# Decoding the gathered tile one tile of gate matrices later, with eight of its gathers among the last parked blocks

## The chip, the cores and the metric

One core of one Trainium2 chip. The time is device microseconds of an execution, the median over several runs. TensorE (PE) does the matmuls, VectorE (DVE) and ScalarE (ACT) the element-wise work, GpSimd (POOL) issues the gathers, and SyncE's queue (SP) issues all other DMAs.

## The reference, cut to what matters

Two transformer blocks over 512 tokens of width 1024, all in float32. What the change touches is the expert layer of the first block (`peer`), for which each of 8 heads chooses 16 of 128 × 128 experts for each token:

```python
q = (xc @ w_query).reshape(c, PEER_HEADS, 2, D_HALF)
sc = jnp.einsum('chpd,hpkd->chpk', q, sub_keys)
sv, si = lax.top_k(sc, PEER_TOPK)
...
fv, fi = lax.top_k(cand, PEER_TOPK)
idx = jnp.take_along_axis(cidx, fi, axis=-1)
g = jax.nn.softmax(fv, axis=-1)
a = jax.nn.gelu(jnp.einsum('chkd,cd->chk', u_tab[idx], xc))
return jnp.einsum('chk,chkd->cd', g * a, v_tab[idx])
```

## The kernel before, in words

The 512 tokens are four tiles of 128. The expert layer does them in two ways.

**Tile 0 is gathered.** Its 128 choices for each token are turned into an index tile `ix` and weights `gw0`. Then 256 gathers follow (`gather_steps`, L482): for each head 16 rows of `u_experts` (tile `gu`, L488) with a dot product on VectorE (L490), a gelu and a product for the head (L493, L494), and 16 rows of `v_experts` (tile `gv`, L497), each added to `hres` by VectorE (L499). Each gather moves 128 rows of 4 KB, 512 KB. They share four buffers, so POOL runs at most four gathers ahead of VectorE.

**Tiles 1 to 3 are computed densely.** All experts' hidden values are made (`h_block`, L469, or `h_stage`, L697: 24 matmuls of 384 columns for a block of 128 experts), multiplied by a gate matrix that is zero where an expert was not chosen, and multiplied with `v_experts` (`v_stage`, L718). The gate matrices are built beforehand (`gate_matrix`, L615), 16 tokens at a time, so eight for each tile, named (t, q): for each token a one-hot column `og` (two instructions on ScalarE at L633 and L634, or one on VectorE at L630, by the table `ON_DVE`), a one-hot block `oj` for eight tokens (VectorE, L620), a matmul for each token (L636), a copy by ScalarE (`stg`, L638) and a store to DRAM (`wdr`, L639).

**Parked blocks.** TensorE has little to do while choices are made and gate matrices are built, so 68 of the 128 hidden blocks are computed there and stored (`park_blocks`, L477): a load of 512 KB, a split into `whi` by ScalarE (L132) and `wlo` by VectorE (L134), 24 matmuls into `hps`, a gelu (`hg`, L474), a store of 192 KB. Sixteen go along with the choices (L545), two with each decode (L574), one or two behind each gate matrix (L640, by `PARKS`), and the rest, four, behind the last (L653).

**Decoding** (`decode`, L564) turns a tile's choices into what its gate matrices or gathers need: comparisons and sums on VectorE (`eq`, L584 to L589), an exponential on ScalarE (L596), whose table load and the load back to the gelu's table (at L474) come with it, and for tile 0 the index tile (L603, L604). It is called for tile 1 ahead of the first gate matrix, and for the others at the places in the table `DECODE`. Once tile 0 is decoded, each gate matrix is followed by `GATH[t]` gathers (L642).

In this stage the order of instructions on each engine is the framework's scheduler's: it takes ready instructions by their order in the program, so that later work can fill gaps that it foresees. The waits on buffers and data are as in the program.

**The long loop** (L743) runs in an order written out by hand: for each of the 128 blocks loads ahead, splits ahead (`dsplit`, L680), a share of the gathers left by `RATE` (0.74 for a parked block, 2.6 for another), the next block's hidden values with the multiplication `hw` (L709), and this block's `v_stage`. The matmuls of the last three blocks come after the loop (L760).

Of the kernel before, what the change touches and what calls it, by code (L numbers as in the profile page):

```python
# [25 lines left out]
PARKED = [n for n in range(NLEAD, 128)  # L26
          if (n + 1 - NLEAD) * NPARK // (128 - NLEAD) > (n - NLEAD) * NPARK // (128 - NLEAD)]
PARKS = ((), (2, 1), (2, 2), (2, 1))
GATH = (0, 1, 3, 3)
RATE = (0.74, 2.6)  # L30
DECODE = {(1, 1): 0, (1, 4): 2, (2, 3): 3}
ON_DVE = ((), (0, 2), (0, 1, 2), (0, 1, 2))
INV_FREQ = [1.0, 0.1939227432012558, 0.03760603070259094, 0.007292664609849453,
            0.0014142135623842478, 0.00027424818836152554, 5.3182957344688475e-05, 1.0313385246263351e-05]
# [9 lines left out]
def body(ctx: ExitStack, tc: tile.TileContext, A: dict, out: bass.AP):  # L44
# [377 lines left out]
    with ExitStack() as st:  # L422
# [54 lines left out]
        def park_blocks():  # L477
            for k, n in enumerate(PARKED):
                SY.dma_start(park[k], h_block(n))
                yield  # L480

        def gather_steps():  # L482
            a = ga
            for h in range(8):
                hs = slice(16 * h, 16 * h + 16)
                for s_ in range(16 * h, 16 * h + 16):
                    u = gt.tile([128, D], F32, name="gu", tag="gu")
                    GP.indirect_dma_start(out=u, out_offset=None, in_=A["u_experts"],  # L488
                                          in_offset=bass.IndirectOffsetOnAxis(ap=ix[:, s_:s_ + 1], axis=0))
                    V.tensor_tensor_reduce(out=u, in0=u, in1=xtok, scale=1.0, scalar=0.0,  # L490
                                           op0=OP.mult, op1=OP.add, accum_out=a[:, s_:s_ + 1])
                    yield
                SC.activation(a[:, hs], a[:, hs], AF.Gelu)  # L493
                V.tensor_tensor(a[:, hs], a[:, hs], gw0[:, hs], op=OP.mult)  # L494
                for s_ in range(16 * h, 16 * h + 16):
                    v = gt.tile([128, D], F32, name="gv", tag="gu")
                    GP.indirect_dma_start(out=v, out_offset=None, in_=A["v_experts"],  # L497
                                          in_offset=bass.IndirectOffsetOnAxis(ap=ix[:, s_:s_ + 1], axis=0))
                    V.scalar_tensor_tensor(hres[:, 0, :], v, a[:, s_:s_ + 1], hres[:, 0, :],  # L499
                                           op0=OP.mult, op1=OP.add)  # L500
                    yield

        parks = park_blocks()
        gathers = gather_steps()

        def spread(gen, n):
            for _ in range(n):
                next(gen, None)

        with mix as s1:  # L510
# [104 lines left out]
            def gate_matrix(t, q, sT, nT):  # L615
                stg = rw.tile([128, 128, TG], F32, name="stg", bufs=2)
                for c in range(TG // 8):
                    t8 = q * TG + 8 * c
                    oj = rw.tile([128, 8, 128], F32, name="oj", bufs=2)
                    V.tensor_tensor(oj, io[:, None, :].to_broadcast([128, 8, 128]),  # L620
                                    sT[:, 1, t8:t8 + 8, None].to_broadcast([128, 8, 128]), op=OP.is_equal)
                    for e in range(2):
                        pool, tag = ((psw, "wps"), (pmm, "mm"))[e]
                        ps = pool.tile([128, 4, 128], F32, name="wps", tag=tag)
                        for k in range(4):
                            tok = t8 + 4 * e + k
                            dve = k in ON_DVE[t]
                            og = rw.tile([128, 128], F32, name="og", tag="ogv" if dve else "oga", bufs=6)
                            if dve:
                                V.tensor_scalar(og, io, sT[:, 0, tok:tok + 1], sT[:, 2, tok:tok + 1],  # L630
                                                op0=OP.is_equal, op1=OP.mult)
                            else:
                                SC.activation(og, io, AF.Abs, bias=nT[:, 0, tok:tok + 1])  # L633
                                SC.activation(og, og, AF.Relu, scale=nT[:, 2, tok:tok + 1],  # L634
                                              bias=sT[:, 2, tok:tok + 1])
                            PE.matmul(ps[:, k, :], lhsT=oj[:, 4 * e + k, :], rhs=og)  # L636
                        o = 8 * c + 4 * e
                        SC.activation(stg[:, :, o:o + 4].rearrange("p i t -> p t i"), ps, AF.Copy)  # L638
                SY.dma_start(wdr[(t - 1) * (128 // TG) + q], stg)  # L639
                spread(parks, PARKS[t][q % 2])  # L640
                if 0 in ahead:
                    spread(gathers, GATH[t])  # L642

# [3 lines left out]
            for t in range(1, NT):  # L647
                for q in range(128 // TG):
                    if (t, q) in DECODE:
                        n = DECODE[t, q]  # L650
                        ahead[n] = decode(n)
                    gate_matrix(t, q, *ahead[t])
            spread(parks, NPARK)  # L653

        dn = st.enter_context(tc.tile_pool(name="dn", bufs=2, reuse_waits="tile"))
# [466 lines left out]
```

## Time and profile before

| | us |
|---|---|
| median of 3 runs | 2280.13 (2277.22 to 2281.48) |
| the profiled execution | 2283.24 |
| its span, first to last instruction | 2281.5 |
| TensorE busy | 2222.8 (97%) |
| VectorE busy | 1500.5 (66%) |
| ScalarE busy | 999.0 (44%) |
| POOL busy | 357.4 (16%) |
| mean granted TensorE clock | 0.991 |

The stage of the gate matrices takes about 545 to 860 us of the span: the store of the first gate matrix is issued at 578.34, that of (2,0) at 678.49, of (3,0) at 784.14, and of the last at 855.04. The long loop follows up to about 1660. Busy times are the union of an engine's instructions; a matmul's end is modelled, so that short gaps between matmuls don't show as idle. The granted clock is a mean over the stretch, in shares of full speed.

### The profile page before, as it was taken

How to read it: one execution, taken by the hardware profiler on the slowest of the kernel's cores; microseconds unless marked ns; L12 is line 12 of the kernel's file. 1: busy time of each engine (PE TensorE's matmuls, PEld its weight loads, DVE VectorE, ACT ScalarE, POOL GpSimd, SP SyncE). 2: the span in 40 equal slices, each digit the busy share in tenths (PEclk: the TensorE clock that was granted, in tenths of full speed). 3: DMA queues.
4: the chain of work that ended last, by engine and by line, in shares of the span. 5: the costliest groups of instructions: out<-in, count | busy, mean ns of one | idle time of the engine just before them, and what ended most of it. 6: DMA issues, size and time to landing. Idle time of an engine off the chain costs nothing.

```text
span 2281.5 us, 30213 instructions
## 1 busy us (share of the span) xinstructions
PE 2222.8 (97%) x11337; PEld 1924.1 (84%) x11337; DVE 1500.5 (66%) x3010; ACT 999.0 (44%) x1655; POOL 357.4 (16%) x261
## 2 busy tenths in 40 slices
PE   7999998999999999999999999999999999999998
PEld 6888887888899998888888888888876778888886
DVE  5663445999999995777777777777774655333323
ACT  5474224333997773333333333333353464323221
POOL 0000000000122421333333333333200000000000
PEclk9999999999999999999999999999999999999999
DMA  4303233443687998989989888988732112333331
GB/s 157 93 29 121 83 95 112 125 123 107 236 313 289 368 334 278 320 296 310 322 303 324 301 311 302 331 317 306 251 112 68 56 61 91 98 95 99 94 101 65
DMA packets 177572, 444.82 MB, mean 195 GB/s; under 512 B 15249, under 2 KB 84241, under 8 KB 174353
## 3 DMA queue, kind: packets, MB, share of 16 engines
q1 hardware_dynamic: 140560, 308.65, 40.3%
q0 software_dynamic: 36864, 134.23, 16.7%
q8 instruction: 89, 1.46, 0.2%
q14 instruction: 59, 0.48, 0.1%
HBM read 402.19 MB, written 40.63 MB: 194 GB/s over the span
## 4 chain that ended last, share of the span: by engine, by line
PE 84%; DVE 6%; ACT 5%; issue 4%; DMA 2%; POOL 0%; SPq 0%; DVEq 0%; ACTq 0%; POOLq 0%
PE mm L138 13%; PE mm L139 13%; PE mm L140 13%; PE acc L138 7%; PE acc L140 7%; PE acc L139 7%; PE hps L140 6%; PE hps L138 6%; PE hps L139 6%; PE wps L636 2%; ACT stg L638 1%; PE pv L363 1%; PE sc L914 1%; PE pv L940 1%; DVE wlo L134 1%
## 5 line engine op out<-in xcount | busy, mean ns | idle before, releaser
L132 ACT ACTIVATE whi<-wraw 128x1024 fp32r<-128x1024 f32 x232 | 241.8, 1045 | 532.6 <-PE mm L139 304.2
L134 DVE TENSOR_TENSOR wlo<-wraw,whi 128x1024 fp32r<-128x1024 f32 x232 | 278.5, 1203 | 271.3 <-ACT whi L132 269.0
L138 PE MATMUL hps<-x2h,whi 128*128 128x384 f32 x1024 | 347.5, 339 | 2.0 <-ACT whi L132 1.8
L140 PE MATMUL hps<-x2h,wlo 128*128 128x384 f32 x1024 | 344.8, 337 | 1.4 <-DVE wlo L134 0.9
L139 PE MATMUL hps<-x2l,whi 128*128 128x384 f32 x1024 | 343.8, 336 | 0.0
L488 POOL DMA_INDIRECT gu<-in_u_experts_dram,ix x128 | 176.7, 1380 | 900.7 <-PE wps L636 584.7
L138 PE MATMUL acc<-whi,hh 128*128 128x512 f32 x768 | 301.4, 392 | 9.4 <-ACT hh L119 9.3
L140 PE MATMUL acc<-whi,hl 128*128 128x512 f32 x768 | 302.7, 394 | 0.6 <-DVE hl L120 0.6
L139 PE MATMUL acc<-wlo,hh 128*128 128x512 f32 x768 | 301.2, 392 | 0.0
L688 DVE TENSOR_TENSOR wlo<-wraw,whi 128x1024 fp32r<-128x1024 f32 x188 | 228.2, 1222 | 84.0 <-ACT whi L686 83.8
L686 ACT ACTIVATE whi<-wraw 128x1024 fp32r<-128x1024 f32 x188 | 196.1, 1052 | 117.5 <-issue 51.9
L497 POOL DMA_INDIRECT gv<-in_v_experts_dram,ix x128 | 178.4, 1394 | 380.7 <-DVE hres L499 264.4
L138 PEld LDWEIGHTS hps<-x2h,whi 128*128 128x128 f32 x1024 | 193.0, 188 | 5.5 <-ACT whi L132 2.1
L139 PEld LDWEIGHTS hps<-x2l,whi 128*128 128x128 f32 x1024 | 192.8, 188 | 2.8
L140 PEld LDWEIGHTS hps<-x2h,wlo 128*128 128x128 f32 x1024 | 192.7, 188 | 2.2 <-DVE wlo L134 1.1
L138 PEld LDWEIGHTS acc<-whi,hh 128*128 128x128 f32 x768 | 144.8, 189 | 42.8 <-ACT hh L119 14.9
L119 ACT ACTIVATE hh<-hw 128x384 fp32r<-128x384 f32 x128 | 67.2, 525 | 248.1 <-DVE hw L709 248.1
L140 PEld LDWEIGHTS acc<-whi,hl 128*128 128x128 f32 x768 | 144.8, 189 | 35.2 <-DVE hl L120 5.3
L139 PEld LDWEIGHTS acc<-wlo,hh 128*128 128x128 f32 x768 | 144.8, 189 | 28.8
L499 DVE SCALAR_TENSOR_TENSOR hres<-gv,ga,hres 128x1024 f32<-128x1024 f32 x128 | 164.0, 1281 | 3.7 <-DMA gv<-in_v_experts_dram,ix 2.4
L490 DVE CUSTOM_DVE_ANT_0 gu<-gu,xtok 128x1024 f32<-128x1024 f32 x128 | 153.9, 1218 | 0.0
L139 PE MATMUL mm<-x4l,whi 128*128 128x512 f32 (+1 forms) x384 | 143.3, 374 | 0.0
(320 smaller groups left out, 4135.4 us busy)
## 6 DMA issues: line engine op xcount, KB each, us to landing
wraw<-in_u_cols_dram SPq DMA_DIRECT2D x128, 512.0 KB, 6.1
wraw<-in_v_experts_dram SPq DMA_DIRECT2D x128, 512.0 KB, 6.0
wraw<-in_w_in_dram SPq DMA_DIRECT2D x50, 512.0 KB, 3.6
wdr<-stg SPq DMA_DIRECT2D x24, 1024.0 KB, 5.3
wt<-wdr SPq DMA_DIRECT2D x16, 1536.0 KB, 11.4
park<-hg SPq DMA_DIRECT2D x68, 192.0 KB, 3.9
hg<-park SPq DMA_DIRECT2D x68, 192.0 KB, 6.2
wraw<-in_w_gate_dram SPq DMA_DIRECT2D x22, 512.0 KB, 3.5
```

The costliest lines, as they stand in the source:

```text
L119: SC.activation(hi, ps, AF.Copy)
L132: SC.activation(hi, raw, AF.Copy)
L134: V.tensor_tensor(lo, raw, f(hi), op=OP.subtract)
L138: PE.matmul(ps, lhsT=ah, rhs=bh, start=start, stop=False)
L139: PE.matmul(ps, lhsT=ah, rhs=bl, start=False, stop=False)
L140: PE.matmul(ps, lhsT=al, rhs=bh, start=False, stop=stop)
L488: GP.indirect_dma_start(out=u, out_offset=None, in_=A["u_experts"], in_offset=bass.IndirectOffsetOnAxis(ap=ix[:, s_:s_ + 1], axis=0))
L490: V.tensor_tensor_reduce(out=u, in0=u, in1=xtok, scale=1.0, scalar=0.0, op0=OP.mult, op1=OP.add, accum_out=a[:, s_:s_ + 1])
L497: GP.indirect_dma_start(out=v, out_offset=None, in_=A["v_experts"], in_offset=bass.IndirectOffsetOnAxis(ap=ix[:, s_:s_ + 1], axis=0))
L499: V.scalar_tensor_tensor(hres[:, 0, :], v, a[:, s_:s_ + 1], hres[:, 0, :], op0=OP.mult, op1=OP.add)
L686: SC.activation(hi, raw, AF.Copy)
L688: V.tensor_tensor(lo, raw, f(hi), op=OP.subtract)
```

## The change

`GATH` is the number of gathers behind each gate matrix of tile t, and `DECODE` names the gate matrix (t, q) ahead of which a tile is decoded. Tile 0's decode moves from (1, 1) to (2, 1), tile 3's from (2, 3) to (2, 4). The gathers behind gate matrices become 3 × 7 + 3 × 8 = 45 where there were 7 + 24 + 24 = 55, and eight more are placed in pairs behind the last four parked blocks. Ahead of the long loop there are then 53 for 55.

```diff
-GATH = (0, 1, 3, 3)
+GATH = (0, 0, 3, 3)
 RATE = (0.74, 2.6)
-DECODE = {(1, 1): 0, (1, 4): 2, (2, 3): 3}
+DECODE = {(1, 4): 2, (2, 1): 0, (2, 4): 3}
...
                     gate_matrix(t, q, *ahead[t])
+            for _ in range(4):
+                spread(parks, 1)
+                spread(gathers, 2)
             spread(parks, NPARK)
```

## Rows read from the trace of the kernel before

**Rows 1.** The page: each engine's busy time, share of the span, instructions.

```profile
PE 2222.8 (97%) x11337; PEld 1924.1 (84%) x11337; DVE 1500.5 (66%) x3010; ACT 999.0 (44%) x1655; POOL 357.4 (16%) x261
```

**Rows 2.** Stretches: length, each engine's busy time (instructions), granted clock, DMA share, GB/s.

```profile
566.00:668.60 102.60, 93.29 (x575) 89.34 (x576) 95.33 (x177) 96.74 (x198) 24.22 (x17) 0.94 0.71 253
584.00:590.00 6.00, 4.61 (x23) 4.14 (x23) 4.72 (x15) 5.90 (x12) 3.89 (x4) 0.65 0.48 137
590.00:596.00 6.00, 6.00 (x33) 6.00 (x32) 6.00 (x12) 5.23 (x14) 3.27 (x2) 0.78 0.87 292
...
723.00:784.00 61.00, 61.00 (x407) 60.62 (x407) 60.86 (x110) 45.62 (x84) 26.70 (x19) 1.00 0.99 361
845.00:860.00 15.00, 15.00 (x99) 14.85 (x98) 6.76 (x11) 7.93 (x10) 1.68 (x1) 1.00 0.84 300
860.00:892.00 32.00, 32.00 (x179) 31.14 (x178) 11.83 (x14) 12.38 (x18) 0.00 (x0) 1.00 0.79 251
```

**Rows 3.** TensorE's waits, 566 to 600, 600 to 683, 683 to 860: total, times, longest.

```profile
PE hps L138 <- ACT whi L132: 1.8, 1, 1.8
PE wps L636 <- DVE og L630: 1.4, 2, 0.9
...
PE wps L636 <- ACT og L634: 5.6, 7, 1.1
...
PE wps L636 <- DVE og L630: 1.0, 3, 0.7
```

**Rows 4.** ScalarE's waits, 566 to 669.

```profile
ACT stg L638 <- PE wps L636: 3.0, 4, 1.9
ACT hg L474 <- PE hps L140: 2.3, 2, 1.3
```

**Rows 5.** VectorE in order of time, at tile 0's and tile 3's decode: start, length.

```profile
572.06 0.22 DVE L577 TENSOR_SCALAR ab<-fi 128x128 uint32<-128x128 uint32 x1
...
582.85 1.25 DVE L620 TENSOR_TENSOR oj<-io,sT 128x1024 f32<-128x1024 f32 x1
...
682.19 0.29 DVE L566 CAST sif<-si 128x256 bf16<-128x256 uint32 x1
...
705.52 0.40 DVE L591 TENSOR_TENSOR sel<-eq 128x128 f32<-128x128 bf16 x1
```

**Rows 6.** Groups of instructions from 540 to 870: count, busy us, mean ns.

```profile
L132 ACT ACTIVATE whi<-wraw 128x1024 fp32r<-128x1024 f32 x49 | 51.4, 1060 | 48.4 <-PE hps L139 47.8
L499 DVE SCALAR_TENSOR_TENSOR hres<-gv,ga,hres 128x1024 f32<-128x1024 f32 x23 | 29.6, 1287 | 0.3
L474 ACT ACTIVATE hg<-hps 128x384 f32<-128x384 f32 x51 | 24.3, 477 | 4.9 <-issue 2.5 <-PE hps L140 2.3
L596 ACT ACT_TABLE_LOAD x4 | 5.1, 1283 | 0.1
L474 ACT ACT_TABLE_LOAD x4 | 5.1, 1283 | 0.1
L596 ACT ACTIVATE gw<-gw 128x128 f32<-128x128 f32 x4 | 1.2, 310 | 3.1 <-DVE gw L595 3.0
```

**Rows 7.** Parked blocks' matmuls in two stretches: PE, PEld and ACT busy (instructions).

```profile
545.00:561.00 16.00, 16.00 (x93) 15.69 (x91) 2.02 (x5) 1.00 0.26 82
566.00:668.60 102.60, 61.72 (x316) 55.60 (x317) 6.28 (x13) 0.94 0.71 253
```

**Rows 8.** The gathers' dot products (L490, two instructions each) up to 680.

```profile
566.00:680.00 114.00, 19.13 (x32) 0.94 0.74 267
```

**Rows 9.** VectorE in order of time, at the end of the long loop.

```profile
1645.93 2.60 DVE L499 SCALAR_TENSOR_TENSOR hres<-gv,ga,hres 128x1024 f32<-128x1024 f32 x2
...
1654.31 1.23 DVE L688 TENSOR_TENSOR wlo<-wraw,whi 128x1024 fp32r<-128x1024 f32 x1 [1.30 <-ACT whi L686]
1655.45 0.55 DVE L709 TENSOR_TENSOR hw<-hg,wt 128x384 f32<-128x384 f32 x1
```

**Rows 10.** TensorE in order of time, at the end of the long loop.

```profile
1656.64 0.50 PE L138 MATMUL acc<-whi,hh 128*128 128x512 f32 x1 [2.10 <-ACT hh L119]
```

## The prediction

> **What bounds the kernel now.** I read the page first, for the engine that the span belongs to [rows 1]: TensorE is marked busy for 97% of it, VectorE for 66%. So a change pays only where TensorE stands still or runs below its rate. The change lies in the stage of the gate matrices (545 to 860 us), so I cut that stage by what TensorE does in it [rows 2]. From 723 to 784, in the second tile (t=2), TensorE is busy in all 61.00 us, at 0.150 us for each of its 407 matmuls. From 566 to 668.6, the first tile (t=1), it is busy 93.29 of 102.60, and 575 matmuls at 0.150 us would take 86.3. So about 16 us are lost there, by idle time, by the lower clock (mean grant 0.94), and by small gaps that the modelled ends cover.
>
> [...]
>
> Who holds TensorE in the first tile? The waits [rows 3] say: up to 600 us, ScalarE's split of a weight once (1.8) and VectorE's one-hot rows (1.4); from 600 to 683, ScalarE's one-hot rows alone (5.6 in 7 waits). ScalarE is busy 96.74 of 102.60 us in this tile [rows 2] and waits for TensorE only 3.0 and 2.3 us [rows 4]. So ScalarE is what this tile runs at, with one place where VectorE was late: the decode of tile 0 occupies VectorE from 572.06 to 582.85, where the one-hot block `oj` of the next gate matrix at last starts [rows 5]. [...] In the second and third tiles VectorE is full (60.86 of 61.00) and TensorE loses nearly nothing; its one wait for VectorE from 683 to 860 is 1.0 us [rows 3].
>
> **The change part by part.**
>
> *Decode of tile 0, and its two parked blocks, out of the first tile.* ScalarE is relieved of two table loads (1.283 each) and an exponential (0.3): 2.9 us. Each of the two parked blocks that the decode issues takes with it a split (1.06) and a gelu (0.48), so 3.1 us [rows 6]. Where ScalarE sets the pace the tile ends 2.9 + 3.1 = 6.0 us earlier. Its two issue DMAs each (a 512 KB load, a 192 KB store) go along on SP's queue; they now stand behind the stores of eight more gate matrices, with nothing but later loads and stores behind them.
>
> *ScalarE's own waits in the first tile.* Of its waits for TensorE [rows 4], 1.9 us is the start of the tile and stays. The others (1.1 for the gate matrices' results, 2.3 for parked blocks) come from TensorE being late. With two parked blocks less it should not be: I take 3.4, the whole, because the waits are for exactly the work that thins out; the ends are 0 and 3.4.
>
> *The same two blocks in the second tile.* There TensorE has no room. A parked block is 24 matmuls at 0.172 us (93 in 16.00) [rows 7], so two cost 2 × 4.13 = +8.3 us. If instead they are taken into the first tile as filler, ScalarE pays 3.1 for them there and the 8.3 is gone. No row shows a parked block running ahead of its place: from 566 to 668.6 there are 316 such matmuls, 13 blocks, and the program places 15 between the first and the last gate matrix of the tile. So I take the full 8.3; the low end is 3.1.
>
> *The decode in its new place.* It needs some 10.8 us of VectorE, from 572.06 to 582.85 [rows 5], in a tile where VectorE is full. What is queued behind it is the next `oj` and `og`, and TensorE behind those. The nearest row is tile 3's decode in the same tile: it began at 682.19, well ahead of its place, and all of TensorE's waits for VectorE in that stretch come to 1.0 us. I take +1.0. The ends are 0 (taken wholly into the first tile) and 6.6: what the decode cost where it stood, 3.2 us of waits (1.8 and 1.4 [rows 3]) and the slow pieces behind them. [...]
>
> *Gathers.* Ten fewer stand ahead of the last parked blocks (45 for 55), so VectorE has some 12 us less to do before them, at 1.2 to 1.3 each; that offsets the decode there. Sixteen dot products ran by 680 [rows 8], where the program had placed ten by the end of the second tile's first gate matrix, so gathers are moved freely into VectorE's gaps, and none held TensorE. I take 0, within −1 and +1. POOL's queue carries nothing but gathers here, so its longer wait for the index tile stops nothing else.
>
> *Eight gathers among the last four parked blocks.* VectorE idles 8.2 of 15 us from 845 to 860 and 20.2 of 32 from 860 to 892 [rows 2]; eight updates at 1.287 [rows 6] are 10.3. They also bring 4.2 MB into 47 us in which the DMA engines are busy 0.84 and 0.79 of the time: 9.1 us are free for 11.6 at the 361 GB/s of the second tile. The 2.5 us over would come late to the long loop's first loads; TensorE has three blocks to do meanwhile, so I take 0, with ends 0 and 2.5.
>
> *Two gathers less before the long loop.* The loop's rate gives 206 places. With 53 done it needs 203 of them, not 201, so one gather falls after block 124's matmuls and one before the multiplication `hw` for block 126. VectorE's idle time before 1654.31 takes the first. The second comes between the split at 1654.31 and `hw` at 1655.45 [rows 9], behind which TensorE already waited 2.10 us at 1656.64 [rows 10]. Two such updates take 2.60, so this is +1.3 us; ends 0 and 2.6.
>
> **Sum:** −6.0 − 3.4 + 8.3 + 1.0 + 0 + 0 + 1.3 = +1.2 us. The profiled execution took 2283.24 (span 2281.5 and 1.7 around it), 3.11 over the median of the runs. So 2284.4 in its terms, and **2281.3** as a median. About 0.2%, 4.6 us, is what a measurement of this kernel can tell from no change, so this is no change.
>
> **The rivals.**
>
> *A: the forecast.* Work moved from a tile that ScalarE limits into one that TensorE limits: gain and cost cancel. For it: ScalarE's 96.74 of 102.60. It also covers a schedule that pulls all of the decode back into the first tile, so that the change does little of what it says; then only the loop's end is left, +1.3, the same time. Chance 0.50.
>
> *B: faster.* VectorE, not ScalarE, is the real brake at the start of the first tile. With the decode gone the stall and its slow clock (6.6) vanish, and 2.9 of the 5.6 us of waits for ScalarE's one-hot rows go with the table loads, while the parked blocks fill holes: −6.6 − 2.9 + 1.3 = −8.2, so 2271.9. For it: 10.8 us in a row in which the next `oj` could not start [rows 5]. Against: ScalarE was busy 5.90 of 6 us from 584 to 590 [rows 2], so its work was not held up with TensorE's. Chance 0.23.
>
> *C: slower.* The decode takes the place it had before, one tile later: run in one piece ahead of `oj` in a tile where VectorE is full, it makes the old stall again, 6.6 for the 1.0 of the sum. +1.2 + 5.6 = +6.8, so 2286.9. It decides at whether `oj` for gate matrix (2,1) starts before or after the decode's comparisons. For it: 60.86 of 61.00 [rows 2]. Against: tile 3's decode was spread from 682.19 to 705.92, other work between [rows 5]. Chance 0.20.
>
> *D: slower by the clock.* The row shows it first: the grant fell to 0.65 [rows 2] behind 3.2 us of waits, and stayed 1.00 in the later stretches, where no wait for ScalarE passed 1.1 us [rows 3]. With two blocks fewer TensorE idles more in the first tile. Two more falls like the one at 584 to 596, each 3.4 us of lost rate (half of 6.8), give +1.2 + 6.8 = +8.0, so 2288.1. Chance 0.07. [...]
>
> **How the numbers follow.** Faster 0.23 is B. The same is A, 0.50, whose own range is 2277 to 2285. Slower 0.27 is C and D. The range reaches from B's time to D's and one us beyond, **2272 to 2289**; the rest of B and the mishaps that join C with D are left out.
>
> **What would show it.** Right: TensorE's loss from 566 to the first tile's end is still 13 to 18 us, ScalarE's share there over 0.93, no 0.65 grant near 584 to 590, the first tile some 8 us shorter and the second some 8 longer; idle TensorE of about 1 us more near 1656. Wrong towards B: the second tile ends at its old time or earlier with the parked blocks in it. Wrong towards C or D: a wait for `og` or `oj` of over 2 us after 683, or a grant under 1.00 there. Wrong altogether: new waits for `wraw` between 700 and 900, which would say that the DMA engines' 0.99 in the second tile had no room.

## The result: slower by 0.6%, and the profile after

| | before | after |
|---|---|---|
| median, on the same chip | 2281.05 us (6 runs) | **2296.85 us** (6 runs) |
| ratio, with 95% interval | | **1.0063** [1.0051, 1.0074] |
| the profiled execution | 2283.24 | 2297.36 |
| its span | 2281.5 | 2295.7 |

The forecast was 2281.3, in a range of 2272 to 2289. The change costs 14 to 16 us, so the forecast of no change was wrong, and the result lies outside the range.

**Where the 14.2 us of the spans are.** I cut both spans at instructions that each kernel has: the store of each tile's last gate matrix, the first multiplication `hw` of the long loop, and its last.

| stretch | before | after | difference |
|---|---|---|---|
| up to the first tile's last store | 669.78 | 665.72 | −4.1 |
| second tile (to its last store) | 102.48 | 119.26 | **+16.8** |
| third tile and the last parked blocks (to the first `hw`) | 107.21 | 106.95 | −0.3 |
| long loop (first to last `hw`) | 778.06 | 778.13 | +0.1 |
| from there to the end | 623.97 | 625.64 | +1.7 |

So in these two spans the first tile did become shorter and the second longer, as forecast, but by 4.1 and 16.8 where the text had 9.4 and 9.3. How the loss divides between the two tiles is less sure than their sum: a second span of the same order of instructions (the last experiment) has +1.8 and +14.5.

The second tile can be read from one view: its stretch in both kernels (length, busy time of PE, PEld, DVE, ACT and POOL with their instructions, granted clock, DMA share, GB/s). First the kernel before, whose rows ahead of the prediction showed only a part of it, then the kernel after.

```profile
669.78:772.26 102.48, 101.62 (x670) 100.37 (x669) 101.11 (x184) 78.62 (x142) 31.98 (x23) 1.00 0.88 321
```

```profile
665.72:784.98 119.26, 111.88 (x709) 110.52 (x708) 109.08 (x189) 81.11 (x146) 45.10 (x29) 0.97 0.89 324
```

Three numbers in these two lines make up the difference. There are 39 more matmuls: those of the two parked blocks, 48, less 9 because the boundary between the tiles falls inside a block in the kernel before. 39 × 0.172 = 6.7 us. TensorE's idle time is 7.4 for 0.9, so +6.5. And the granted clock is 0.97 for 1.00: an estimate of what that loses is 0.03 × 119.26 = 3.6 (0.6 either way by the rounding of the grant). Together 16.8.

What made TensorE idle there? VectorE in order of time, after (start, length; in brackets the idle time ahead of it and what ended it):

```profile
718.33 1.24 DVE L620 TENSOR_TENSOR oj<-io,sT 128x1024 f32<-128x1024 f32 x1
...
720.00 2.61 DVE L499 SCALAR_TENSOR_TENSOR hres<-gv,ga,hres 128x1024 f32<-128x1024 f32 x2
722.53 1.22 DVE L134 TENSOR_TENSOR wlo<-wraw,whi 128x1024 fp32r<-128x1024 f32 x1
723.66 2.64 DVE L499 SCALAR_TENSOR_TENSOR hres<-gv,ga,hres 128x1024 f32<-128x1024 f32 x2
726.22 1.22 DVE L134 TENSOR_TENSOR wlo<-wraw,whi 128x1024 fp32r<-128x1024 f32 x1
728.35 1.29 DVE L499 SCALAR_TENSOR_TENSOR hres<-gv,ga,hres 128x1024 f32<-128x1024 f32 x1 [0.91 <-DMA gv<-in_v_experts_dram,ix]
731.02 1.29 DVE L499 SCALAR_TENSOR_TENSOR hres<-gv,ga,hres 128x1024 f32<-128x1024 f32 x1 [1.39 <-DMA gv<-in_v_experts_dram,ix]
733.67 1.28 DVE L499 SCALAR_TENSOR_TENSOR hres<-gv,ga,hres 128x1024 f32<-128x1024 f32 x1 [1.36 <-DMA gv<-in_v_experts_dram,ix]
734.87 1.22 DVE L134 TENSOR_TENSOR wlo<-wraw,whi 128x1024 fp32r<-128x1024 f32 x1
736.00 2.60 DVE L499 SCALAR_TENSOR_TENSOR hres<-gv,ga,hres 128x1024 f32<-128x1024 f32 x2
738.52 1.62 DVE L630 TENSOR_SCALAR og<-io,sT 128x128 f32<-128x128 f32 x6
```

Nine gather updates (L499) stand in VectorE's queue between the one-hot block at 718.33 and the next one-hot rows at 738.52. The first four go at 1.3 us each. After that the four buffers that were ready are used up, and the next ones start 2.65 us apart (728.35, 731.02, 733.67), each waiting for its rows to land. The `og` rows behind them use nothing that an update makes, and their six buffers come free with the matmuls at 733.45 below; they stand behind the updates in VectorE's order and start at 738.52. TensorE, in order of time, shows the price:

```profile
733.45 1.95 PE L636 MATMUL wps<-og,oj 128*128 128x128 f32 x16
739.01 2.88 PE L636 MATMUL wps<-og,oj 128*128 128x128 f32 x16 [3.61 <-DVE og L630]
```

In this span the clock follows: the six microseconds in which TensorE waits, the next six, and the same at a second place, where VectorE waits 2.6 us for one gather ahead of `og` rows.

```profile
732.00:738.00 6.00, 3.40 (x27) 3.17 (x25) 4.61 (x5) 4.18 (x7) 3.06 (x3) 1.00 0.94 364
738.00:744.00 6.00, 4.99 (x25) 5.00 (x26) 6.00 (x16) 3.40 (x7) 2.40 (x2) 0.72 0.94 349
762.00:768.00 6.00, 4.01 (x30) 3.85 (x30) 3.45 (x9) 3.74 (x6) 2.32 (x3) 0.96 0.97 343
768.00:774.00 6.00, 6.00 (x32) 6.00 (x32) 6.00 (x11) 4.00 (x8) 0.00 (x0) 0.76 0.72 262
```

TensorE was busy 3.40 and 4.01 of 6 us, and the pieces behind were granted 0.72 and 0.76. Such a fall does not come each time: in the second span of the same order TensorE was busy 3.24 of 6 us at the first of these places, and the piece behind it was granted 1.00.

```profile
738.00:744.00 6.00, 3.24 (x26) 3.01 (x24) 4.44 (x4) 4.19 (x7) 3.12 (x3) 1.00 0.99 345
744.00:750.00 6.00, 5.13 (x35) 5.15 (x36) 6.00 (x16) 3.84 (x9) 2.26 (x2) 1.00 0.97 356
```

The waits of TensorE after, 566 to 683 and 683 to 870 (in all, times, longest), answer to [rows 3]:

```profile
PE wps L636 <- ACT og L634: 10.3, 13, 1.4
PE wps L636 <- DVE og L630: 1.2, 1, 1.2
...
PE wps L636 <- DVE og L630: 6.0, 4, 3.6
```

For ScalarE's rows they rose from 5.8 over the same stretch to 10.3, and for VectorE's rows in the second and third tiles from 1.0 to 6.0.

**The decode did not stay where it was put.** On VectorE the kernel's scheduler took tile 0's decode back into the first tile, some 40 to 50 us later than it had been, and tile 3's decode began there too (VectorE in order of time):

```profile
612.08 0.18 DVE L569 TENSOR_SCALAR over<-fi 128x128 uint32<-128x128 uint32 x1
...
632.71 0.22 DVE L604 CAST ix<-ixf 128x128 int32<-128x128 f32 x1
632.84 0.22 DVE L569 TENSOR_SCALAR over<-fi 128x128 uint32<-128x128 uint32 x1
```

The first gather is issued at 633.88 for 585.19 before. Tile 0's two parked blocks were not taken back: TensorE does 39 fewer of such matmuls by the end of the first tile. The eight gathers meant for the last parked blocks were taken forward into the third tile: POOL's last issue before the long loop is at 844.73. ScalarE's switches to the exponential and back were in the first tile three times (at 609.86, 620.68 and 656.55), where there had been two:

```profile
609.86 1.28 ACT L596 ACT_TABLE_LOAD   x1
...
620.68 1.28 ACT L596 ACT_TABLE_LOAD   x1
...
656.55 1.28 ACT L596 ACT_TABLE_LOAD   x1
```

The end of the loop is as forecast. VectorE runs one more update ahead of the last but one `hw`, and TensorE's wait for `hh` (the upper part of `hw`) is 3.3 where it was 2.10 [rows 10]:

```profile
1665.65 1.23 DVE L691 TENSOR_TENSOR wlo<-wraw,whi 128x1024 fp32r<-128x1024 f32 x1 [0.59 <-ACT whi L689]
1666.79 1.28 DVE L499 SCALAR_TENSOR_TENSOR hres<-gv,ga,hres 128x1024 f32<-128x1024 f32 x1
1667.99 0.55 DVE L712 TENSOR_TENSOR hw<-hg,wt 128x384 f32<-128x384 f32 x1
```

```profile
PE acc L138 <- ACT hh L119: 3.3, 1, 3.3
```

### The profile page after: what moved, and what is told of

Its sections match the earlier page's. It is cut to its first block, busy times and chain, and to the rows that moved or that the text cites. A ratio compares the mean times of both kernels' runs of the same rounds, so it can differ in the third digit from the quotient of the medians.

```text
span 2295.7 us, 30213 instructions
## 1 busy us (share of the span) xinstructions
PE 2226.7 (97%) x11337; PEld 1925.5 (84%) x11337; DVE 1503.1 (65%) x3010; ACT 999.4 (44%) x1655; POOL 362.5 (16%) x261
## 4 chain that ended last, share of the span: by engine, by line
PE 80%; DVE 6%; issue 5%; ACT 4%; DMA 4%; POOL 0%; SPq 0%; DVEq 0%; POOLq 0%; ACTq 0%
PE mm L138 13%; PE mm L139 13%; PE mm L140 13%; PE acc L138 6%; PE acc L140 6%; PE acc L139 6%; PE hps L140 5%; PE hps L138 5%; PE hps L139 5%; PE wps L636 2%; DMA wraw<-in_u_cols_dram 1%; ACT stg L638 1%; DMA gv<-in_v_experts_dram,ix 1%; PE pv L363 1%; PE sc L917 1%
## 5 line engine op out<-in xcount | busy, mean ns | idle before, releaser
L138 PEld LDWEIGHTS acc<-whi,hh 128*128 128x128 f32 x768 | 144.9, 189 | 44.8 <-ACT hh L119 16.8
L499 DVE SCALAR_TENSOR_TENSOR hres<-gv,ga,hres 128x1024 f32<-128x1024 f32 x128 | 164.1, 1282 | 7.2 <-DMA gv<-in_v_experts_dram,ix 6.0
L490 DVE CUSTOM_DVE_ANT_0 gu<-gu,xtok 128x1024 f32<-128x1024 f32 x128 | 154.3, 1222 | 2.8 <-DMA gu<-in_u_experts_dram,ix 2.8
```

The lines of the kernel that those rows point to most:

```text
L138: PE.matmul(ps, lhsT=ah, rhs=bh, start=start, stop=False)
```

## The experiments

Two questions came out of this: which of the moved things costs (tile 0's decode, its two parked blocks, tile 3's decode, the eight gathers), and whether the run of updates is what holds the second tile. Ratios are to the kernel before on the same chip, with 95% intervals. Stretches are those of the table above, as differences from the kernel before, taken from each kernel's one profiled span; the long loop alone varies by some 3 us either way from span to span (774.56 to 781.42 from its first `hw` to its last, over the kernels here), so I compare stretches and medians, not spans. In the two spans of one order the first tile differs by 5.9 us and the second by 2.2, so differences of that size between single spans decide nothing by themselves.

### The parked blocks at their old places

The changed kernel, with the blocks of the decodes issued at (1,1), (1,4) and (2,3) as before.

```diff
-                    spread(parks, 1)
+                    spread(parks, t in (1, 2))
...
+                    if (t, q) in ((1, 1), (2, 3)):
+                        spread(parks, 2)
```

> The changed kernel, but the six parked blocks that the decodes of tiles 0, 2 and 3 bring stand where they stood before: two ahead of gate matrix (1,1), two at (1,4), two at (2,3). The decodes themselves stay at the new places. Theory T (two costs: about 5.5 us because the first tile of gate matrices has two parked blocks less to fill TensorE while ScalarE sets the pace; about 7 us because nine gather updates in a row stand on VectorE ahead of one-hot rows of the second tile, more than the four gather buffers, so that they run at the pace of landing; and some 1.3 us at the end of the long loop): the first cost goes, the run of nine stays (now ahead of (2,3)), so about 2291, 10 over the kernel before. Rival R (53 gathers in a shorter time fill the DMA engines, wherever anything stands): no change against the changed kernel, about 2297.

Measured: 2286.82, ratio 1.0018 [1.0009, 1.0028]. The late place of the blocks makes 1.0063 − 1.0018, 0.45% or some 10 us, of the change: about twice what the theory had for it, and the rival, for which the transfers were the cost, falls. The first tile is −0.8, the second +4.5. This kernel moves tile 3's two blocks back by one gate matrix as well; the next pair moves tile 0's alone.

### Tile 3's blocks spread, without and with that

Tile 3's two parked blocks behind gate matrices (2,4) and (2,5) in place of within the decode, so that the longest run of updates is six in place of nine; then the same with tile 0's blocks at (1,1).

```diff
-                    spread(parks, 1)
+                    spread(parks, t != 3)
...
                     gate_matrix(t, q, *ahead[t])
+                    spread(parks, (t, q) in ((2, 4), (2, 5)))
```

> The changed kernel, but the two parked blocks of tile 3's decode stand one behind gate matrix (2,4) and one behind (2,5), so that no four parked blocks lie between two gate matrices and the longest run of gather updates ahead of one-hot rows is six instead of nine. Theory T: the second cost shrinks to some 2 us or less, the first stays: about 2290 to 2292, and VectorE's waits for gather landings between 700 and 790 fall from 6.3 us to under 3. Rival R: no change, about 2297, with the waits for landings as they were.

> The changed kernel with both: tile 0's two parked blocks back ahead of (1,1), tile 3's two spread behind (2,4) and (2,5); decodes and gathers as in the changed kernel. Theory T: only the end of the long loop and rests are left, 2282 to 2286, within 5 us of the kernel before. Rival R: about 2297.

Measured: 2299.95, ratio 1.0066 [1.0046, 1.0085], and 2288.12, 1.0023 [1.0013, 1.0033]. Both missed the theory: the spreading gained nothing. It did not take the waiting away, it only divided it. VectorE has two runs here that end in a wait (six updates from 740.06, and five with a dot product from 759.84), and from 690 to 870 it waits 7.1 us for gathers to land, for 6.3 in the changed kernel. The pair gives the price of tile 0's two blocks, 0.43%.

### Tile 3's decode alone

```diff
-DECODE = {(1, 1): 0, (1, 4): 2, (2, 3): 3}
+DECODE = {(1, 1): 0, (1, 4): 2, (2, 4): 3}
```

> The kernel before with one part of the change: tile 3 decoded ahead of (2,4) instead of (2,3), tile 0 and the gathers as before. The longest run of gather updates is six. Theory T: the first tile is untouched, the run of six costs little: 2281 to 2284. Rival R2 (the move of tile 3's decode alone puts four parked blocks and its comparisons where VectorE is fullest): 2287 or more.

Measured: 2286.2, ratio 1.0012 [1.0001, 1.0022], between the two theories. In its trace the second tile is +4.3: its matmuls are 670 as before, but TensorE idles 3.1 us, and the clock is 0.97. One gate matrix's delay of this decode is enough to bring a run of six updates and a wait of 2.9 us for `og`. This is the cleanest case of the runs: in its second tile VectorE has the same instructions as before (one split more) and TensorE the same number of matmuls, so the 4.3 us (2.2 of idle time and a grant of 0.97) come with nothing but the order.

```profile
668.99:775.73 106.74, 103.63 (x670) 103.05 (x669) 101.43 (x185) 78.75 (x142) 31.86 (x23) 0.97 0.87 308
```

### The parked blocks alone

The kernel before, with only the blocks of the decodes moved to the changed kernel's places.

```diff
-                    spread(parks, 1)
+                    spread(parks, t in (1, 2))
...
+                    if (t, q) in ((2, 1), (2, 4)):
+                        spread(parks, 2)
```

> Theory T1 (the parked blocks that the decodes issue, taken later, are what lengthens the first two tiles: about 10 us by the difference of the two kernels with and without them at their old places): the kernel before with nothing but these blocks moved is slower by 6 to 12 us, about 0.3 to 0.5%; the stores of gate matrices (2,0) to (2,7) come later than before, no run of gather updates over four on VectorE, and no new wait of TensorE for VectorE over 2 us. Rival T2 (the blocks' place costs only together with the decode that ran beside them): within 3 us of the kernel before.

Measured: 2290.28, ratio 1.0033 [1.0021, 1.0045], 7.5 us: theory T1 on the time. The first tile is −4.6, the second +11.4. Its part about runs and waits missed: there is a run of eight updates too, and one wait of 2.5. The second tile's row (46 more matmuls than before; idle 113.90 − 110.79 = 3.1 for 0.9) gives 46 × 0.172 = 7.9 for the blocks, 2.2 for the idle time, and 1.1 for a clock of 0.99:

```profile
665.20:779.10 113.90, 110.79 (x716) 110.03 (x715) 109.96 (x198) 81.65 (x147) 38.89 (x29) 0.99 0.89 324
```

### The updates held behind the one-hot rows

This asks what the second tile takes without the runs. In the changed kernel each gather's instructions are put behind the last VectorE `og` of the gate matrix that they are issued after. Up to the end of the second tile this leaves TensorE's order as it was; on VectorE the updates come later, and 20 of them fall in the second tile in place of 28. Then the same with both moves of parked blocks.

```diff
-                    spread(gathers, GATH[t])
+                    with tc.issue_after(pin[0].ins):
+                        spread(gathers, GATH[t])
```

> The changed kernel, with each gather update put behind the last VectorE one-hot row of its gate matrix in VectorE's order (nothing waits for more than before). Theory G (a run of nine gather updates that go at the pace of their landings holds the one-hot rows, and costs 4 to 5 us in the second tile): 4 to 5 us below the changed kernel, about 2291 to 2293, the waits of VectorE for landed gathers from 690 to 870 under 1 us and TensorE's longest wait for a one-hot row of VectorE there under 1.5 us; the cost of the later parked blocks stays. Rival P (the run stands where VectorE would be late anyway, and the time is the second tile's fuller TensorE and VectorE): within 2 us of the changed kernel, with the wait for one-hot rows gone to other places.

> The decodes' parked blocks of tile 0 at their old place, tile 3's spread, and gather updates kept behind the one-hot rows. Theory G: 2281 to 2284, no difference from the kernel before beyond the loop's end (1.3 us). Rival P: as the same kernel without the order, about 5 us slower than before, ratio 1.002.

Measured: 2305.49, ratio 1.0101 [1.0086, 1.0117], and 2300.56, 1.0084 [1.007, 1.0098]. On the time, theory G missed in both, and so did its rival. In the second tile theory G is right, though. Its stretch in the first of the two, and in the second:

```profile
667.03:776.68 109.65, 108.24 (x708) 106.90 (x706) 88.37 (x164) 80.94 (x146) 31.45 (x19) 1.00 0.84 296
776.68:904.33 127.65, 114.48 (x725) 111.63 (x725) 103.73 (x181) 74.88 (x127) 57.09 (x35) 0.98 0.95 337
```

```profile
669.04:771.25 102.21, 100.45 (x664) 99.45 (x663) 84.69 (x161) 76.99 (x141) 30.37 (x19) 1.00 0.84 298
```

Without the runs the second tile takes 109.65 in place of 119.26, at full clock, with no wait for `og` from 683 to 800. With the blocks back at their old place too, it takes 102.21: the 102.48 of the kernel before. So of the 16.8 us in the second tile 7.4 (109.65 − 102.21) go with the two parked blocks, and 9.6 with what the hold took out: the runs of updates, the clock that followed in that span, and the work of eight updates (10.3 us of VectorE, which is idle 10.2 us of the changed kernel's second tile). Against the second span of the changed kernel's order, where the clock stayed at 1.00, the 9.6 are 7.4. This experiment does not part the order from the amount of work; that order alone costs is shown by the kernel with tile 3's decode alone.

But the gathers that VectorE no longer takes there come later. From 776.68 to the first `hw` (second line) POOL issues 35, for 17 in the changed kernel from its second tile's end, the DMA engines are 0.95 busy, and the stretch is 20.4 us longer than before. ScalarE's and TensorE's waits from 850 to 905 say how:

```profile
ACT whi L132 <- DMA wraw<-in_u_cols_dram: 16.8, 3, 8.7
ACT whi L692 <- DMA wraw<-in_v_experts_dram: 12.1, 2, 11.9
```

```profile
PE hps L138 <- ACT hg L711: 6.4, 1, 6.4
PE hps L138 <- ACT hg L474: 6.1, 3, 3.2
```

Weights land late. ScalarE waits to split them, the gelus `hg` of blocks that are already computed stand behind in its queue (for TensorE's results it waits only 1.7 us there), and TensorE waits for the `hps` buffers that they free.

### One more one-hot row on VectorE in the first tile

By the prediction ScalarE is what the first tile runs at, so I gave one of its rows to VectorE: three of four in place of two. Four kernels: with both moves of parked blocks and the updates held; with both moves alone; the kernel before with nothing else; and that with both moves and the eight gathers issued in the third tile in place of among the last blocks (`GATH = (0, 0, 3, 4)`).

```diff
-ON_DVE = ((), (0, 2), (0, 1, 2), (0, 1, 2))
+ON_DVE = ((), (0, 1, 2), (0, 1, 2), (0, 1, 2))
```

> As the kernel with both, and in the first tile one more one-hot row of every four on VectorE in place of ScalarE. If ScalarE sets the first tile's pace (97 of 103 us busy in the kernel before), the first tile is shorter by 4 to 10 us and the whole 2272 to 2279. If the first tile's pace is as much VectorE's (66 of 103 us busy, but the decode of one or two tiles in it), the waits of TensorE go from ScalarE's rows to VectorE's and the time is 2280 to 2288.

> The changed kernel with tile 0's parked blocks at their old place, tile 3's spread, and one more one-hot row of every four on VectorE in the first tile; nothing of the order of the gather updates is forced. Theory G2 (the pinned kernels lost at the stage's end what they won in the second tile, because gathers came late): without the force the gate matrices end 8 to 12 us earlier than in the same kernel with the old rows, the stage's end has no wait for hg over 2 us, and the time is 2274 to 2280. Rival: VectorE full in both tiles, 2284 to 2290.

> The kernel before with one more one-hot row of every four on VectorE in place of ScalarE in the first tile. In the pinned kernel with this edit the eight gate matrices of the first tile were stored by 656.9 for 669.0. If ScalarE alone sets the first tile's pace, this gives 6 to 12 us here too: 2271 to 2277. If VectorE, which must also run two decodes there, takes over, the time is within 4 us of before.

> The kernel with old and spread parked blocks and one more one-hot row of four on VectorE, its eight gathers no longer among the last parked blocks but issued as a fourth per gate matrix of the third tile. Theory H (gathers at the stage's end delay the landing of the long loop's first V weights; ScalarE's split of those stands ahead of the last parked block's gelu, so TensorE waits 6.7 us for hg): ScalarE's wait for the V weights' landing from 860 to 905 falls from 9.9 to under 3 us, TensorE's wait for hg to under 2, and the time to 2277 to 2282. Rival K (VectorE's work in the stage is what is conserved; the wait moves): within 2 us of 2287, with new waits for one-hot rows in the third tile.

| | median | ratio | first tile | second | third and last blocks |
|---|---|---|---|---|---|
| both, held | 2290.09 | 1.0028 [1.0016, 1.004] | −12.9 | +4.1 | +19.0 |
| both | 2287.34 | 1.0034 [1.0021, 1.0047] | −12.6 | +6.6 | +8.3 |
| the kernel before | 2282.41 | 1.001 [0.9998, 1.0022] | +1.2 | −1.8 | −0.2 |
| both, gathers in the third tile | 2286.94 | 1.0025 [1.0015, 1.0035] | −12.9 | +6.4 | +13.2 |

With tile 0's decode started later, the first tile is 12.6 us shorter. In the kernel before the row wins nothing, though ScalarE's busy time falls to 77.45 of 104.95 us there, from 97.92 of 103.78:

```profile
566.00:670.95 104.95, 92.65 (x582) 90.98 (x582) 96.76 (x198) 77.45 (x136) 15.80 (x13) 0.92 0.67 236
```

```profile
PE hps L138 <- ACT hg L474: 6.4, 3, 5.4
PE wps L636 <- DVE og L630: 5.9, 3, 4.4
```

TensorE waits 5.9 us for VectorE, which has that decode to run (4.4 of it ahead of 600), and 6.4 for gelus on ScalarE, which itself waits 13.1 us for weights to land. But the 12.6 us are all given back. In the second kernel ScalarE waits 9.9 us for one landing of the long loop's first V weights, and TensorE 6.7 us for `hg`. With the eight gathers earlier (the last kernel) these fell to 2.3 and 3.7, as theory H had it; yet TensorE's waits for VectorE's `og` rose from 1.2 to 4.4, ScalarE waited 6.6 for another load, and the time is the same within the intervals. The rival K is right about the time. None of these beats the kernel before.

### The eight gathers alone, and tile 0's decode alone

First the kernel before with the four added lines alone.

```diff
+            for _ in range(4):
+                spread(parks, 1)
+                spread(gathers, 2)
             spread(parks, NPARK)
```

> The kernel before with nothing but eight gathers issued among the last four parked blocks (two fewer stand behind the loop's first blocks than there were, as in the changed kernel). Theory L (the one part of the forecast that came out: one more gather update ahead of the last multiplication of the long loop): 1 to 1.5 us slower than before, the wait of TensorE for hh at the loop's end 3.3 us where it was 2.1, the gate-matrix stage as before. Rival M (the eight gathers cost in the stage of the gate matrices, since VectorE takes them among its one-hot rows): 3 us or more, with a wait for one-hot rows of over 2 us between 700 and 860.

Measured: 2288.1, ratio 1.0034 [1.0021, 1.0047]. Neither theory: the wait for `hh` stayed at 2.1 (eight more gathers ahead of the loop leave fewer for it, not more, so that expectation had the sign of its own change wrong), and no wait for `og` passed 1.2. The first two tiles are as before; the stretch from there to the first `hw` is +4.2. ScalarE's and TensorE's waits there, 850 to 900:

```profile
ACT whi L689 <- DMA wraw<-in_v_experts_dram: 7.0, 2, 6.3
```

```profile
PE hps L138 <- ACT hg L474: 2.5, 1, 2.5
```

That is the case the prediction bounded with 2.5 us, "late to the long loop's first loads". It happens when the gathers do run at that place.

Then the kernel before with tile 0's decode at (2,1), its two parked blocks staying at (1,1), and no gathers among the last blocks (so `GATH` is again (0, 0, 3, 3)).

```diff
-GATH = (0, 1, 3, 3)
+GATH = (0, 0, 3, 3)
...
-DECODE = {(1, 1): 0, (1, 4): 2, (2, 3): 3}
+DECODE = {(1, 4): 2, (2, 1): 0, (2, 3): 3}
```

> The kernel before with nothing but tile 0's decode one tile later, its two parked blocks staying where they were. Theory S (the scheduler takes the decode back into the first tile, about 40 us later than before, so that gathers begin at 630 to 640 for 585 and come closer together in the second tile): the first tile ends as before within 3 us, the waits of VectorE for landed gathers between 690 and 870 are 2 us or more, and the whole is 1 to 4 us slower. Rival N (decode 0 alone is free, the loss is of decode 3's place): within 1 us of before.

Measured: 2303.39, ratio 1.01 [1.0085, 1.0114], 23 us. Theory S is right about the stage (first tile −0.9, second +5.9, third +1.4) and far off in sum, for a reason that the rows at the end give. With 45 gathers ahead of the loop and 206 places in it, five of 256 are left over, and they run after the last matmul of the loop with TensorE waiting for their sum:

```profile
PE tr L150 <- DVE xs L783: 12.1, 2, 11.5
```

So the eight gathers at the stage's end are not an extra of the change but what makes the later decode bearable: without them the end of the loop costs 14.7 us more.

### The eight gathers in the third tile

The changed kernel, and the one with both moves of parked blocks, with `GATH = (0, 0, 3, 4)` and without the four lines.

> The changed kernel with the eight gathers as a fourth per gate matrix of the third tile in place of among the last parked blocks. In the changed kernel's trace these gathers were issued by 845 already and no load waited at the stage's end, so Theory H gives no difference: 2295 to 2299, within 2 us of the changed kernel. Rival K: 3 us or more slower or faster.

> The changed kernel with tile 0's parked blocks at their old place, tile 3's spread, and the eight gathers as a fourth per gate matrix of the third tile. Theory H, as for the changed kernel: no difference from the same kernel with them among the last blocks, ratio to before 1.001 to 1.003. Rival K: outside that.

Measured: 2295.91, ratio 1.0061 [1.0046, 1.0075], and 2286.48, 1.0021 [1.0011, 1.0031]: no difference from 1.0063 and 1.0023, as expected. In the changed kernel these gathers had run in the third tile all along.

The first of the two tells more. Its instructions stand in the same order as the changed kernel's on TensorE, VectorE, ScalarE and GpSimd, from the first to the last, and so do SyncE's DMAs. It is a second span of the same order. Its stretches are +1.8, +14.5, +0.8, −0.1 and +0.1. The first tile in the kernel before, in the changed kernel and here, and the second tile here:

```profile
566.00:669.78 103.78, 94.47 (x582) 90.53 (x583) 96.45 (x178) 97.92 (x200) 24.22 (x17) 0.94 0.72 255
566.00:665.72 99.72, 87.14 (x537) 79.72 (x537) 88.67 (x174) 96.44 (x197) 18.50 (x12) 0.97 0.59 210
566.00:671.59 105.59, 93.20 (x544) 86.00 (x545) 90.99 (x178) 96.53 (x197) 17.37 (x12) 0.90 0.56 203
671.59:788.62 117.03, 108.75 (x706) 107.09 (x705) 107.69 (x188) 80.85 (x146) 40.74 (x29) 1.00 0.91 323
```

Between the two spans of one order the grant of the first tile is 0.97 or 0.90, and that of the second 0.97 or 1.00. TensorE's idle time in the second tile is there in both, 7.4 and 8.3 us.

## Why the prediction was wrong

**What bounds the stage** was read rightly for the second tile, TensorE, and only in part for the first. One row less on ScalarE shortened the first tile by 12.6 us where VectorE had room. In the kernel before, on which the forecast rests, it shortened it by nothing: VectorE with the decode, and weights that land late, stand close behind ScalarE.

**Decode of tile 0 and two blocks out of the first tile (−6.0), ScalarE's own waits (−3.4).** The first tile was 4.1 shorter, not 9.4, and in the second span 1.8 longer. The first step that failed: the 2.9 us of table loads and exponential did not go. The scheduler brought the decode back to 612, and drew tile 3's exponential in with it, so ScalarE has one such pair more there, not one less. Its busy time fell by 1.5 us (97.92 to 96.44) in place of 6.0. Its idle time fell from 5.9 to 3.3 us, 2.6 of the 3.4, in one span, and rose to 9.1 in the other, at the grant of 0.90. The prediction had seen that pull as possible, but counted it only under rival A, with a neutral outcome. The blocks alone gave 4.6 (the kernel with the blocks alone), for which the sum had 3.1 and up to 3.4. And the pieces granted 0.65 and 0.78 at 584 to 596, which the text put down to tile 0's decode and priced into 6.6, came back in the second span (0.68 and 0.75), where that decode had gone to 616 and tile 2's stood in its place, and not in the first span of the same order (1.00 and 1.00); they were not the price of that decode alone. Of the 6.6 (which B and C use), 3.2 are waits [rows 3]; the other 3.4 (D has them twice) were the author's estimate from the grants, (0.35 + 0.22) × 6, and no run shows them as such. What the kernel before shows there is 24 one-hot matmuls in 5.41 us at a grant of 0.50, 0.225 each, and behind them, at a grant of 1.00, 26 in 2.82 us, 0.108 each (TensorE in order of time). By that 24 × 0.117 = 2.8 us are lost in those 24:

```profile
586.63 5.76 PE L636 MATMUL wps<-og,oj 128*128 128x128 f32 x24 [0.85 <-DVE og L630]
592.04 0.67 PE L140 MATMUL hps<-x2h,wlo 128*128 128x384 f32 x1
...
596.21 3.06 PE L636 MATMUL wps<-og,oj 128*128 128x128 f32 x26
599.03 0.42 PE L140 MATMUL hps<-x2h,wlo 128*128 128x384 f32 x1
```

**The two blocks in the second tile (+8.3).** Right in kind and nearly in size: 6.7 by count of matmuls in the changed kernel, 7.4 by the two kernels with held updates. With the 4.6 they give back in the first tile (one span, and less than the 5.9 by which two spans of one order differ), the later blocks should cost 3 us. They cost 7.5 (alone) to 10 (in the changed kernel). Moved alone they bring a run of updates too, 3.3 us of idle time and clock. In the changed kernel that is not the reason, as its run of nine is there with the blocks at their old places too (from 702.9); why they cost 10 there is not shown.

**The decode's new place (+1.0, ends 0 and 6.6) and the gathers (0, within −1 and +1).** This is the step that failed most: "gathers are moved freely into VectorE's gaps, and none held TensorE". That was true of the kernel before, whose runs are at most four updates, as many as there are buffers. In the changed kernel the scheduler put nine in a row in front of one-hot rows. Past the fourth they go at the pace of landings, 2.65 us. In place of +1.0 + 0 stand the 9.6 us of the experiment with held updates (7.4 against the second span), of which the order alone, in the kernel with tile 3's decode alone, shows 4.3 for a shorter run. (The 1.0 us that the text calls one wait are three in [rows 3], the longest 0.7.) Rival C had the stretch and the sign (a wait for `og` of over 2 us after 683, and a grant under 1.00), not the cause: it expected the decode's own instructions to stand in the way. Rival D's mechanism, idle TensorE and then pieces at a low grant, took place too: in the first span in the second tile behind VectorE, in the second span in the first tile, where D had it (0.50 and 0.76 from 608 to 620). The order was the same both times, so the order of instructions alone does not decide which tile it is.

**Eight gathers (0, ends 0 and 2.5).** Right at 0 here, for the wrong reason: they were taken forward, away from the place that was costed. Where they do run there, in the kernel before, they cost 7.6 us, above the upper end.

**Two gathers less before the loop (+1.3).** Right: 3.3 for 2.1 at the place named, in both spans. The stretch after the loop is +1.7 in the first and +0.1 in the second.

In the first span the misses are 5.3 in the first tile, 7.5 in the second and 0.4 at the end, less 0.2 elsewhere: the 13.0 between +1.2 and +14.2. The chance of 0.27 for slower came from C and D; the range ended at 2289 because C was priced with one stall and D with two falls of the clock, and neither with the blocks costing more than their matmuls.

**What stays open.** Why the scheduler orders nine updates in a row once the decode or the blocks come later was not tried. Nor is the cost of the runs parted exactly from that of the work in them. And no kernel tried here is faster than the one before: each gain in one tile came back in the next, first as one-hot rows behind updates, then as late loads.

## What to carry to other kernels

When work is moved in a kernel whose order a scheduler makes, ask of each engine's queue not how much it has to do but what will stand in front of the rows that the bounding engine waits for, and whether those in front can themselves be late. Here a run of nine updates with four buffers came to go at the pace of the transfers (three starts 2.65 us apart, for an update of 1.28), and the one-hot rows behind it started at 738.52, with TensorE waiting 3.61 us for them. And look for what the moved work's consumers do at the far end: in one kernel here five gathers that found no place cost 14.7 of 21 us.

## What was unexpected in the hardware's behaviour

- Gathers of 512 KB taken one after the other, with four buffers and the DMA engines 0.94 busy with these and with weight loads, were ready every 2.65 us; an update takes 1.28.
- The same order of instructions, run twice, was granted 0.97 or 0.90 of the clock in the first tile and 0.97 or 1.00 in the second, and its two spans differ by 5.9 us in the first tile.
- ScalarE's queue turned one late landing (11.9, 9.9 or 6.3 us) into a wait of TensorE for a gelu (6.4, 6.7 and 2.5 us). In the last of the three that gelu ran at 882.53, behind two splits of the late weights at 879.82 and 881.57.
